# A two-layer trunk on one core: the norm's column sums behind the fourth product, half of the operand sums made as x tiles come, turns of h apart from their use, slots oldest first

## The chip, the core and the metric

The kernel runs on one core of a Trainium2 chip. A core has five engines that follow programs of their own and meet at semaphores: TensorE (PE; its weight loads are listed as PEld), VectorE (DVE), ScalarE (ACT), GpSimd (POOL) and SyncE (SP), which here issues nearly all transfers. PE writes into eight banks of PSUM, each 128 partitions by 512 fp32. The metric is the device time of one execution in microseconds (us), lower is better.

## The reference

The input x is 512 positions by 1024 channels, fp32. Two layers follow each other, and a norm ends the program:

```
for layer in range(2):
    h = rmsnorm(x, norm_mix_g[layer])
    x = x + (rglru_mixer(h) if layer == 0 else stick_breaking(h))      # both end with @ w_out
    h = rmsnorm(x, norm_ffn_g[layer])
    x = x + (silu(h @ w_gate) * (h @ w_up)) @ w_down                   # d_ff = 2816
return rmsnorm(x, final_g)
rmsnorm(x, g) = x * rsqrt(mean(x*x, channels) + 1e-6) * g
```

The mixer of layer 0 is a gated linear recurrence with a short convolution; that of layer 1 is attention with 16 heads in blocks of 128 queries.

## The kernel before

**Layout.** x lies transposed in SBUF as eight tiles x_1 to x_8 of 128 channels by 512 positions. Each large matmul in fp32 accuracy is made of three: the high part of one operand (rounded, `wh`, `oh`, `hh`, `uh`) by the high part of the other, high by low and low by high (the low parts `wl`, `ol`, `hl`, `ul` are what the rounding left). Weights come in chunks of 128x1024 from HBM by SP; ACT casts a chunk to its high part (L233), DVE or POOL subtracts to get the low part (L234). Three pairs of buffers and a fourth for every fourth chunk hold them.

**FFN.** `ffn` (L590) works on units of 512 columns of gate and up, u = 0 to 5, the last with 256. A unit is computed by a scheme of seven products in place of eight (in the order 1, 5, 6, 3, 7, 2, 4), each of two chunks and 24 matmuls. The products need sums and differences: of the weights (`source`, L76, made by DVE from the pieces `raw` and `b`, results `tt` or `b` itself), and of the quarters of x (`ffn_in`, L328). For m < 4, `ffn_in` makes one operand tile, for m >= 4 it scales x_(m-3) and x_(m+1) on ACT (L344, L345), makes four sums of 256 columns on DVE (L346, L331), and three high and low parts (L353, L331). `ffn_in` runs for each x tile as the mixer's out product delivers it: PE fills a bank, DVE adds it to x (L585 in layer 0, L970 in layer 1), then the operands are made. `norm_sq` (L371) squares the tile on ACT and adds it to `acc`, on POOL, the last one on DVE. `norm_rs1` sums acc's columns with four small matmuls (L389) and makes the factor rsT, which is needed only where product 2 is scaled (L690).

**h.** A unit's result h lies in the tiles u2 and b5 (L691, L697). In the next unit, `turn` transposes it: for two f tiles, eight transposes into banks 6 and 7 (L627), a copy to hh on ACT (L630), hl on DVE (L631). Then four `down_pair`s (L647) of 24 matmuls (L640 to L642) each use all four hh and hl, go to the banks 6 and 7, and DVE adds these to two x tiles (L645). In unit u the order is: product 1, turn(0,1), product 5, turn(2,3), pair 0, product 6, pair 1, product 3, pair 2, product 7, pair 3, products 2 and 4. In the last unit pairs 2 and 3 are replaced by work behind the units: two down chunks into four banks, turn(0,1) of the last h, then two short chunks that finish the x tiles.

**What sets the order.** PE's order in `ffn` is as written. The orders of DVE, ACT and POOL in `ffn` and in RG-LRU come from a scheduler, so that a change of PE's text moves rows on other engines; attention is written out by hand. Two scratch lists, `free` and `free2`, hand out slots of 128x512 (`new`, `rel`): the main list is served first, in order of release. The table in `plan` sets the order in which SP loads the chunks and the splitting follows. `finish` (L400) ends the program in two halves of the positions: last x add, square, column sums (L411), factor, output.

Of the kernel before, what the change touches and what calls it, by code (L numbers as in the profile page):

```python
# [97 lines left out]
class Kern:  # L98
    def __init__(self, ctx, tc, a, out):
# [6 lines left out]
        self.free = deque(range(NS1))  # L106
        self.free2 = deque()
        self.keep2 = 0
# [15 lines left out]
    @contextmanager  # L124
    def stage(self, name):
        with self.tc.tile_pool(name=name, bufs=1) as self.ar2:
            self.free2 = deque(range(NS1, NS1 + NS2))
            yield
            assert len(self.free2) == NS2
            self.free2 = deque()  # L130

    def new(self, name, dt=F32, second=False, shape=None):
        if second and self.free2:
            i = self.free2.popleft()
        elif self.free or len(self.free2) <= self.keep2:
            i = self.free.popleft()
        else:
            i = self.free2.popleft()
        self.tn += 1
        ar = self.ar if i < NS1 else self.ar2  # L140
        t = ar.tile(shape or [P, S], dt, tag=f"s{i}", bufs=1, name=f"{name}_{self.tn}")
        self.slot[id(t)] = (i, t)
        return t

    def rel(self, *ts_):
        for t in ts_:
            i = self.slot.pop(id(t))[0]
            (self.free if i < NS1 else self.free2).append(i)
# [5 lines left out]
    def plan(self):  # L154
# [173 lines left out]
    def ffn_in(self, m, g):  # L328
# [3 lines left out]
        if m == 0:  # L332
            self.ops = [None] * 4
        if m < 4:
            t = self.new("a11", F32R)
            nc.scalar.activation(t[:, lo], self.x[m][:, lo], AF.Copy, scale=self.col(g, m))
            nc.vector.scalar_tensor_tensor(t[:, hi], self.x[m][:, lo], self.col(g, m), t[:, lo].bitcast(F32),
                                           ALU.mult, ALU.subtract)
            self.ops[m] = {1: (t[:, lo], t[:, hi])}
            self.held.append(t)  # L340
        else:
            k = m - 4
            ua, ub, w1, w2 = (self.tmp() for _ in range(4))
            nc.scalar.activation(ub, self.x[m], AF.Copy, scale=self.col(g, m))  # L344
            nc.scalar.activation(ua, self.x[k], AF.Copy, scale=self.col(g, k))  # L345
            nc.vector.tensor_tensor(w1[:, lo], ua[:, hi], ub[:, hi], ALU.add)  # L346
# [3 lines left out]
            for src, q0, q1 in ((w1, 5, 6), (w2, 7, 3), (ub, 2, 4)):  # L350
                h, l = self.new("oh", F32R), self.new("ol", F32R)
                self.held += [h, l]
                nc.scalar.copy(h, src)  # L353
                sub(l, src, h.bitcast(F32))
                self.ops[k][q0] = (h[:, lo], l[:, lo])
                self.ops[k][q1] = (h[:, hi], l[:, hi])
        self.norm_sq(m)
# [74 lines left out]
    def rglru(self):  # L432
        nc, tc = self.nc, self.tc
        with ExitStack() as cx:
# [146 lines left out]
            ys = list(zip(ah, al))  # L581
            for m in range(KT):
# [7 lines left out]
    def ffn(self, l, gnext):  # L590
        nc, tc = self.nc, self.tc
        mm = nc.tensor.matmul
        with tc.tile_pool(name=f"ffn{l}", bufs=1) as self.fp, tc.manual_schedule(engines={mybir.EngineType.PE}):
# [30 lines left out]
            def turn(fs, banks):  # L624
                for f, b in zip(fs, banks):
                    for t in range(NT):
                        nc.tensor.transpose(b[:, ts(t)], (u2 + b5)[t][:, ts(f)], self.ident)  # L627
                    h, lw = (self.fp.tile([P, S], F32R, tag=f"{n}{f}", bufs=1, name=f"{n}{f}_{self.used}")
                             for n in ("hh", "hl"))
                    nc.scalar.copy(h, b)  # L630
                    nc.vector.tensor_tensor(lw, b, h.bitcast(F32), ALU.subtract)  # L631
                    hh[f] = (h, lw)
# [20 lines left out]
            for u in range(NU + 1):  # L653
                un = self.unit_of()
                w = un.w
                A, B, D = (ab[(u + i) % 3] for i in range(3))
# [18 lines left out]
                if 0 < u < NU:  # L675
                    down_pair(1)
# [3 lines left out]
                if u > 0:  # L680
                    down_pair(2 if u < NU else 1)
# [3 lines left out]
                if 0 < u < NU:  # L685
                    down_pair(3)
# [7 lines left out]
                for j in range(2):  # L694
# [3 lines left out]
                                                   ALU.mult, ALU.mult)  # L698
            self.rel(*self.held)
            self.held = []  # L700
            open_ = {4: tb[0], 5: tb[1], 6: B[0], 7: B[1]}
            w = self.chunk()
            for i in range(2):
                down(w, i, 4, open_[4 + i], last=False)
            save = hh[:]
            split7 = gnext is None
            w = self.chunk()
            hs = (slice(0, HS), slice(HS, S))
            p7 = (B[1], D[0])
            if split7:  # L710
                down(w, 0, 4, open_[6], last=False)
                for p, cs in zip(p7, hs):
                    down(w, 1, 4, p, last=False, cs=cs)
            else:
                for i in range(2):
                    down(w, i, 4, open_[6 + i], last=False)
            turn((0, 1), (A[0], A[1]))
            if gnext is None:
                with tc.issue_after(self.last.ins):
                    nc.scalar.activation(self.st[:, 0:1], self.ones[:, 0:1], AF.Sqrt)  # L720
            fin = [D[1], A[0], A[1], D[1]] if split7 else [D[0], D[1], A[0], A[1]]
            for e in range(2):
                w = self.chunk()
                for i in range(4):
                    m = 4 * e + i
                    if m == KT - 1 and split7:
                        for j in range(2):
                            down(w, i, 2, p7[j], first=False, cs=hs[j])
                            self.bi = 4 + 2 * j
# [5 lines left out]
                    self.norm_in(m, gnext)  # L735
# [374 lines left out]
```

## Time and profile before

| | us |
|---|---|
| median of 3 runs (lowest, highest) | 1240.68 (1239.98, 1242.27) |
| the profiled execution | 1241.45 |
| its span | 1239.7 |
| PE busy, share of the span | 1149.1, 93% |
| DVE busy | 878.8, 71% |
| ACT busy | 640.5, 52% |
| POOL busy | 349.4, 28% |
| one middle unit of the FFN (307 to 371 us): PE busy of 64 us | 62.48 |

The mean granted clock of PE is 0.969 of full speed. The span by stage: RG-LRU up to about 165 us, FFN of layer 0 up to 530, attention up to 850, FFN of layer 1 up to 1218, final norm to the end. In the time line, a row gives start, length, engine, line, operation, output<-inputs, shapes, and in brackets how long the engine stood before it and what ended that. Lengths of neighbouring rows overlap a little, since an engine starts an instruction before the one ahead has retired.

### The profile page before, as it was taken

What the parts mean: (1) busy time and instruction counts of PE and PEld (TensorE: products, weight loads), DVE (VectorE), ACT (ScalarE), POOL (GpSimd) and SP (SyncE); (2) the same over time, 40 slices, a digit from 0 to 9 for tenths busy, and PEclk for the clock granted to TensorE, in tenths of its full rate; (3) what the DMA queues carried; (4) which work ended last, traced back from release to release, by engine and by line L of the source; (5) the groups of instructions that cost most, each with busy time, mean ns of one, the idle gap of its engine ahead of it and who ended that gap; (6) DMA issues with size and microseconds to landing.
All of it is one profiled execution on the core that took longest, in us unless ns stands there. A gap on an engine that the chain in (4) does not pass through costs nothing. (4 is left out here: it accounts for less than half of the span.)

```text
span 1239.7 us, 14201 instructions
## 1 busy us (share of the span) xinstructions
PE 1149.1 (93%) x5363; PEld 946.8 (76%) x5363; DVE 878.8 (71%) x1105; ACT 640.5 (52%) x919; POOL 349.4 (28%) x218
## 2 busy tenths in 40 slices
PE   9999959999999999999989888797999999999995
PEld 6877848787878788888767677675878787878884
DVE  7878696756575756454899999969675757575744
ACT  6697464535353534344677777646353535353432
POOL 2541410111111111351466566621011111111134
PEclk9999989999999999999999999898999999999997
DMA  7223333232324131322111100023324241422101
GB/s 239 85 84 94 109 105 104 83 120 71 134 68 136 68 102 51 103 85 69 51 37 50 34 35 35 34 87 118 102 72 132 68 136 68 137 68 102 51 17 68
DMA packets 30740, 105.83 MB, mean 85 GB/s; under 512 B 3536, under 2 KB 4560, under 8 KB 30672
## 3 DMA queue, kind: packets, MB, share of 16 engines
q1 hardware_dynamic: 30384, 104.40, 25.2%
q8 instruction: 42, 0.69, 0.2%
q10 hardware_dynamic: 288, 0.52, 0.1%
q14 instruction: 26, 0.21, 0.1%
HBM read 102.81 MB, written 2.10 MB: 85 GB/s over the span
## 5 line engine op out<-in xcount | busy, mean ns | idle before, releaser
L234 POOL TENSOR_TENSOR wl<-raw,wh 128x1024 fp32r<-128x1024 f32 (+1 forms) x74 | 180.8, 2443 | 694.6 <-ACT wh L233 692.3
L233 ACT CAST wh<-raw 128x1024 fp32r<-128x1024 f32 (+1 forms) x154 | 156.0, 1017 | 198.6 <-PE bank L622 93.8
L620 PE MATMUL bank<-wh,oh 128*128 128x512 f32 (+1 forms) x576 | 217.0, 377 | 0.0
L621 PE MATMUL bank<-wl,oh 128*128 128x512 f32 (+1 forms) x576 | 215.7, 375 | 0.0
L622 PE MATMUL bank<-wh,ol 128*128 128x512 f32 (+1 forms) x576 | 215.6, 374 | 0.0
L640 PE MATMUL bank<-hh,wh 128*128 128x512 f32 (+1 forms) x358 | 139.9, 391 | 15.6 <-DVE hl L631 15.1
L645 DVE TENSOR_TENSOR x<-x,bank 128x512 f32<-128x512 f32 x87 | 59.7, 686 | 114.5 <-PE bank L642 113.4
L641 PE MATMUL bank<-hl,wh 128*128 128x512 f32 (+1 forms) x358 | 138.6, 387 | 0.4 <-DVE hl L631 0.4
L642 PE MATMUL bank<-hh,wl 128*128 128x512 f32 (+1 forms) x358 | 138.4, 387 | 0.0
L234 DVE TENSOR_TENSOR wl<-raw,wh 128x1024 fp32r<-128x1024 f32 (+1 forms) x80 | 102.1, 1280 | 45.3 <-ACT wh L233 45.2
L622 PEld LDWEIGHTS bank<-wh,ol 128*128 128x128 f32 x576 | 109.6, 190 | 19.3
L620 PEld LDWEIGHTS bank<-wh,oh 128*128 128x128 f32 x576 | 109.8, 191 | 18.8
L621 PEld LDWEIGHTS bank<-wl,oh 128*128 128x128 f32 x576 | 109.7, 190 | 19.0
L233 ACT CAST wh<-tt 128x1024 fp32r<-128x1024 f32 x66 | 69.5, 1053 | 93.2 <-PE bank L622 46.0
L233 ACT CAST wh<-b 128x1024 fp32r<-128x1024 f32 x44 | 46.4, 1053 | 127.6 <-PE bank L622 44.8
L267 PE MATMUL bank<-uh,wh 128*128 128x512 f32 x256 | 104.6, 409 | 6.8 <-DVE t L814 4.3
L268 PE MATMUL bank<-ul,wh 128*128 128x512 f32 x256 | 101.6, 397 | 0.3 <-DVE ul L323 0.3
L269 PE MATMUL bank<-uh,wl 128*128 128x512 f32 x256 | 101.3, 396 | 0.0
L234 DVE TENSOR_TENSOR wl<-tt,wh 128x1024 fp32r<-128x1024 f32 x66 | 80.9, 1225 | 22.0 <-ACT wh L233 21.7
L640 PEld LDWEIGHTS bank<-hh,wh 128*128 128x128 f32 x358 | 67.5, 189 | 31.5 <-DVE hl L631 17.5
L234 DVE TENSOR_TENSOR wl<-b,wh 128x1024 fp32r<-128x1024 f32 x44 | 53.9, 1224 | 41.8 <-ACT wh L233 41.2
L641 PEld LDWEIGHTS bank<-hl,wh 128*128 128x128 f32 x358 | 67.5, 189 | 14.3 <-DVE hl L631 1.1
(205 smaller groups left out, 2328.4 us busy)
## 6 DMA issues: line engine op xcount, KB each, us to landing
raw<-w_gu SPq DMA_DIRECT2D x44, 512.0 KB, 3.5
b<-w_gu SPq DMA_DIRECT2D x44, 512.0 KB, 3.5
raw<-w_dn SPq DMA_DIRECT2D x44, 512.0 KB, 3.5
raw<-w_qk SPq DMA_DIRECT2D x16, 512.0 KB, 3.4
raw<-w_in SPq DMA_DIRECT2D x14, 512.0 KB, 3.9
raw<-w_ao SPq DMA_DIRECT2D x8, 512.0 KB, 3.9
raw<-w_v SPq DMA_DIRECT2D x8, 512.0 KB, 3.5
raw<-w_bo SPq DMA_DIRECT2D x8, 512.0 KB, 3.5
```

The costliest lines, as they stand in the source:

```text
L233: self.nc.scalar.copy(wh[:, c], raw[:, c])
L234: self.wl_engine(i).tensor_tensor(wl[:, c], raw[:, c], wh[:, c].bitcast(F32), ALU.subtract)
L267: mm(out, lhsT=wh, rhs=xh, start=first, stop=False)
L268: mm(out, lhsT=wh, rhs=xl, start=False, stop=False)
L269: mm(out, lhsT=wl, rhs=xh, start=False, stop=last)
L620: mm(out[j][:, :w], lhsT=oh[:, ts(j)], rhs=wh[:, ws], start=st, stop=False, skip_group_check=True)
L621: mm(out[j][:, :w], lhsT=oh[:, ts(j)], rhs=wl[:, ws], start=False, stop=False, skip_group_check=True)
L622: mm(out[j][:, :w], lhsT=ol[:, ts(j)], rhs=wh[:, ws], start=False, stop=en, skip_group_check=True)
L640: mm(out, lhsT=w[0][:, ws], rhs=h[:, cs], start=st, stop=False, skip_group_check=True)
L641: mm(out, lhsT=w[0][:, ws], rhs=lw[:, cs], start=False, stop=False, skip_group_check=True)
L642: mm(out, lhsT=w[1][:, ws], rhs=h[:, cs], start=False, stop=en, skip_group_check=True)
L645: nc.vector.tensor_tensor(self.x[m], self.x[m], bank, ALU.add)
```

## The change

1. `norm_rs1` of unit 0 stands behind product 3, the fourth, and no longer behind product 1.
2. `ffn_in` makes half of the operand sums of product 7 for m < 4, and from m = 4 on three 256-wide sums and one half-wide low part. It scales the older x tile first, and takes its tiles from the main list. All additions to acc go to POOL, in the last norm to DVE.
3. From unit 2 on, turn(0,1) stands ahead of product 1 and turn(2,3) behind it; pair 3 goes behind product 4, ahead of that turn. Pairs 1 and 2 go behind products 3 and 7. Unit 1 keeps its turns. The last turn(0,1) goes between the two down chunks, into tiles of its own. The table of chunks follows.
4. Out tiles of attention use bank m for tile m, and the three pairs of banks of the products are shifted by one pair in layer 1.
5. Slots carry the time of their release; of the two lists the one with the older slot is served.

```diff
-    def new(self, name, dt=F32, second=False, shape=None):
-        if second and self.free2:
-            i = self.free2.popleft()
-        elif self.free or len(self.free2) <= self.keep2:
-            i = self.free.popleft()
+    def new(self, name, dt=F32, second=False, shape=None, first=False):
+        two = not first and len(self.free2) > (0 if second else self.keep2)
+        if two and (second or not self.free or self.free2[0][0] < self.free[0][0]):
+            i = self.free2.popleft()[1]
         else:
-            i = self.free2.popleft()
+            i = self.free.popleft()[1]
...
-                    order = (0, 1, d[0], 2, d[1], 3, d[2], 4, d[3], 5, 6)
+                    order = (0, 1, d[0], 2, 3, d[1], 4, d[2], 5, 6, d[3])
...
+        def split(dst, src):
+            h, l = dst
+            nc.scalar.copy(h, src)
+            sub(l, src, h.bitcast(F32))
+
         if m < 4:
-            t = self.new("a11", F32R)
-            nc.scalar.activation(t[:, lo], self.x[m][:, lo], AF.Copy, scale=self.col(g, m))
-            nc.vector.scalar_tensor_tensor(t[:, hi], self.x[m][:, lo], self.col(g, m), t[:, lo].bitcast(F32),
-                                           ALU.mult, ALU.subtract)
-            self.ops[m] = {1: (t[:, lo], t[:, hi])}
...
+            ua, w2 = self.tmp(), self.tmp()
+            t, t3 = self.new("a11", F32R, first=True), self.new("s3", F32R, first=True)
+            nc.scalar.activation(ua, self.x[m], AF.Copy, scale=self.col(g, m))
+            sub(w2[:, lo], ua[:, lo], ua[:, hi])
+            self.ops[m] = {1: (t[:, lo], t[:, hi]), 7: (t3[:, lo], t3[:, hi])}
+            split(self.ops[m][1], ua[:, lo])
+            split(self.ops[m][7], w2[:, lo])
         else:
...
+            nc.scalar.activation(ua, self.x[k], AF.Copy, scale=self.col(g, k))
             nc.scalar.activation(ub, self.x[m], AF.Copy, scale=self.col(g, m))
-            nc.scalar.activation(ua, self.x[k], AF.Copy, scale=self.col(g, k))
             nc.vector.tensor_tensor(w1[:, lo], ua[:, hi], ub[:, hi], ALU.add)
             sub(w1[:, hi], w1[:, lo], ua[:, lo])
-            sub(w2[:, lo], ua[:, lo], ua[:, hi])
...
+            split((h1, l1), w1)
             sub(w2[:, hi], ub[:, lo], w1[:, hi])
...
+            split(self.ops[k][3], w2[:, hi])
+            split((h2, l2), ub)
-        self.norm_sq(m)
+        self.norm_sq(m, nc.gpsimd)
...
+            self.bi = 0
             for m in range(KT):
...
-                A, B, D = (ab[(u + i) % 3] for i in range(3))
+                A, B, D = (ab[(u + i + l) % 3] for i in range(3))
+                if u > 1:
+                    turn((0, 1), tb)
                 product(1, un, A, 0)
...
-                if u == 0:
-                    self.bi = 6
-                    self.norm_rs1(False)
-                else:
-                    turn((0, 1), tb)
+                if u > 0:
+                    turn((0, 1) if u == 1 else (2, 3), tb)
                 product(5, un, B, 0)
-                if u > 0:
+                if u == 1:
                     turn((2, 3), tb)
...
-                if 0 < u < NU:
-                    down_pair(1)
                 product(3, un, B, 0, False)
...
                 if u > 0:
-                    down_pair(2 if u < NU else 1)
+                    down_pair(1)
+                if u == 0:
+                    self.bi = 6
+                    self.norm_rs1(False)
                 product(7, un, A, 0, False)
...
                 if 0 < u < NU:
-                    down_pair(3)
+                    down_pair(2)
                 product(2, un, D, 0)
...
+                if 0 < u < NU:
+                    down_pair(3)
...
             for i in range(2):
                 down(w, i, 4, open_[4 + i], last=False)
-            save = hh[:]
...
+            nh = [(self.new("h4", F32R), self.new("l4", F32R)) for _ in range(2)]
+            turn((0, 1), (A[0], A[1]), nh)
             w = self.chunk()
...
-                    self.norm_in(m, gnext)
+                    if split7:
+                        self.norm_sq(m, nc.vector)
+                    else:
+                        self.norm_in(m, gnext)
```

Three places of DVE's order show what the scheduler makes of it. The first is behind the last x add of layer 0's mixer, where the last operands and the first weights of product 5 are made (t, ol, ow: sums and low parts of the operands; tt: weight sum; wl: its low part). Before:

```order
L331 TENSOR_TENSOR t_1438<-t_1435 128x256
L331 TENSOR_TENSOR t_1437<-t_1437,t_1435 128x256
L331 TENSOR_TENSOR ol_1454<-t_1436,oh_1453 128x512
L76 TENSOR_TENSOR tt_1485<-b_178_1473,raw_1244 128x1024
L331 TENSOR_TENSOR t_1438<-t_1436,t_1437 128x256
L76 TENSOR_TENSOR tt_1503<-b_179_1475,raw_1300 128x1024
L234 TENSOR_TENSOR wl_1488<-tt_1485,wh_1487 128x1024
L331 TENSOR_TENSOR ol_1446<-t_1437,oh_1445 128x512
```

Now:

```order
L332 TENSOR_TENSOR ow_1468<-t_1458,ow_1467 128x512
L332 TENSOR_TENSOR t_1460<-t_1458,t_1459 128x256
L332 TENSOR_TENSOR ow_1466<-t_1459,ow_1465 128x512
L76 TENSOR_TENSOR tt_1505<-b_186_1493,raw_1272 128x1024
L332 TENSOR_TENSOR ow_1469<-t_1460,ow_1469 128x256
L76 TENSOR_TENSOR tt_1523<-b_187_1495,raw_1326 128x1024
L235 TENSOR_TENSOR wl_1508<-tt_1505,wh_1507 128x1024
```

Two 512-wide low parts stand ahead of the first weight sum, where there was one, and none is left behind wl.

The second is the start of unit 3 of layer 0: the last h tile (b), the last two x adds, the first turn's hl. Before:

```order
L697 SCALAR_TENSOR_TENSOR b_1471<-b_1471,rsT,t_2629 128x512
L76 TENSOR_TENSOR tt_2635<-b_223_2573,tt_2635 128x1024
L234 TENSOR_TENSOR wl_2656<-tt_2653,wh_2655 128x1024
L697 SCALAR_TENSOR_TENSOR b_1472<-b_1472,rsT,t_2632 128x512
L76 TENSOR_TENSOR tt_2653<-b_224_2597,tt_2653 128x1024
L234 TENSOR_TENSOR wl_2709<-tt_2635,wh_2708 128x1024
L631 TENSOR_TENSOR hl_80_2678<-bank_76,hh_80_2677 128x512
L631 TENSOR_TENSOR hl_80_2686<-bank_77,hh_80_2685 128x512
```

Now:

```order
L706 SCALAR_TENSOR_TENSOR b_1491<-b_1491,rsT,t_2617 128x512
L235 TENSOR_TENSOR wl_2672<-tt_2669,wh_2671 128x1024
L706 SCALAR_TENSOR_TENSOR b_1492<-b_1492,rsT,t_2620 128x512
L654 TENSOR_TENSOR x_7_84<-x_7_84,bank_76 128x512
L76 TENSOR_TENSOR tt_2669<-b_231_2585,tt_2669 128x1024
L654 TENSOR_TENSOR x_8_85<-x_8_85,bank_77 128x512
L235 TENSOR_TENSOR wl_2690<-tt_2687,wh_2689 128x1024
L639 TENSOR_TENSOR hl_78_2658<-bank_76,hh_78_2657 128x512
L639 TENSOR_TENSOR hl_78_2666<-bank_77,hh_78_2665 128x512
```

The two x adds of pair 3 have come between b and hl, with a weight sum between them.

The third is unit 1, whose turns keep their place. Before:

```order
L631 TENSOR_TENSOR hl_44_1822<-bank_77,hh_44_1821 128x512
L76 TENSOR_TENSOR tt_1771<-raw_1931,tt_1771 128x1024
L234 TENSOR_TENSOR wl_1880<-tt_1789,wh_1879 128x1024
L631 TENSOR_TENSOR hl_46_1865<-bank_76,hh_46_1864 128x512
L631 TENSOR_TENSOR hl_46_1873<-bank_77,hh_46_1872 128x512
```

Now:

```order
L639 TENSOR_TENSOR hl_44_1842<-bank_77,hh_44_1841 128x512
L76 TENSOR_TENSOR tt_1789<-raw_1933,tt_1789 128x1024
L235 TENSOR_TENSOR wl_1898<-tt_1807,wh_1897 128x1024
L76 TENSOR_TENSOR tt_1807<-raw_1951,tt_1807 128x1024
L235 TENSOR_TENSOR wl_1930<-b_199_1729,wh_1929 128x1024
L639 TENSOR_TENSOR hl_46_1883<-bank_76,hh_46_1882 128x512
L639 TENSOR_TENSOR hl_46_1891<-bank_77,hh_46_1890 128x512
```

One weight sum and one low part more stand ahead of the second turn's hl.

More of the change, by code (lines that the diff above doesn't have):

```diff
@@ L105, in __init__ @@
         self.ar = mk("ar", 1)
-        self.free = deque(range(NS1))
+        self.free = deque((0, i) for i in range(NS1))
         self.free2 = deque()
+        self.clock = 0
         self.keep2 = 0
@@ L126, in stage @@
         with self.tc.tile_pool(name=name, bufs=1) as self.ar2:
-            self.free2 = deque(range(NS1, NS1 + NS2))
+            self.free2 = deque((0, i) for i in range(NS1, NS1 + NS2))
             yield
@@ L704, in ffn @@
                 down(w, i, 4, open_[4 + i], last=False)
-            save = hh[:]
-            split7 = gnext is None
+            nh = [(self.new("h4", F32R), self.new("l4", F32R)) for _ in range(2)]
+            turn((0, 1), (A[0], A[1]), nh)
             w = self.chunk()
[L708 to L721, printed above, removed]
+            down(w, 0, 4, open_[6], last=False)
+            for p, cs in zip(p7, hs) if split7 else ((open_[7], slice(0, S)),):
+                down(w, 1, 4, p, last=False, cs=cs)
+            hh[:2] = nh
+            fin = [D[1], A[0], A[1], D[1] if split7 else D[0]]
             for e in range(2):
```

35 lines of the change are left out of this document (21 added, 14 removed).

## The prediction

> **What bounds the kernel now.** I read the page first: one engine is busy nearly all the time.
>
> ```profile
> span 1239.7 us, 14201 instructions
> PE 1149.1 (93%) x5363; PEld 946.8 (76%) x5363; DVE 878.8 (71%) x1105; ACT 640.5 (52%) x919; POOL 349.4 (28%) x218
> ```
>
> TensorE (PE) bounds the kernel. The change keeps the number of its matmuls, so only what PE loses between them can be won: idle time, and time at half its clock. The view of waits says who ends the idle time (total, times, longest, in us); the window below it is attention.
>
> ```profile
> PE bank L389 <- DVE acc L371: 17.9, 2, 13.2
> PE bank L640 <- DVE hl L631: 15.1, 10, 1.5
> PE bank L627 <- DVE b L697: 4.9, 4, 1.6
> PE bank L620 <- DVE x L970: 4.3, 1, 4.3
> ...
> 530.00:795.00 265.00, 238.88 (x1163) 193.06 (x1161) 226.28 (x316) 181.17 (x304) 144.52 (x104) 0.96 0.15 50
> ```
>
> The first row is the norm's column sums, twice; the second and third are the turns of h, spread over five units of two layers; the fourth is the first product of layer 1. Together they are 42 of the 90.6 us (1239.7 less 1149.1) that PE is not busy. Another 26 (265 less 238.88) lie in attention, where the written order is untouched. Last I read the time lines of PE and DVE around each wait. Behind product 1 of layer 0 (start, length; in brackets the idle time before and what ended it):
>
> ```profile
> 165.31 0.39 PE L620 MATMUL bank<-wh,a 128*128 128x512 f32 x1
> 170.52 0.39 PE L622 MATMUL bank<-wh,a 128*128 128x512 f32 x1
> 184.06 1.86 PE L389 MATMUL bank<-ones,acc 128*128 128x1 f32 x8 [13.15 <-DVE acc L371]
> 185.79 0.77 PE L620 MATMUL bank<-wh,oh 128*128 128x512 f32 x1
> 193.76 0.39 PE L620 MATMUL bank<-wh,oh 128*128 128x512 f32 x1
> ...
> 163.48 0.68 DVE L585 TENSOR_TENSOR x<-x,bank 128x512 f32<-128x512 f32 x1
> 167.25 1.52 DVE L331 TENSOR_TENSOR t<-t,t 128x256 f32<-128x256 f32 x1
> 170.07 0.68 DVE L585 TENSOR_TENSOR x<-x,bank 128x512 f32<-128x512 f32 x1
> 172.22 0.43 DVE L346 TENSOR_TENSOR t<-t,t 128x256 f32<-128x256 f32 x1 [1.47 <-ACT t L345]
> 173.83 1.22 DVE L76 TENSOR_TENSOR tt<-b,raw 128x1024 f32<-128x1024 f32 x1
> 176.44 1.22 DVE L234 TENSOR_TENSOR wl<-tt,wh 128x1024 fp32r<-128x1024 f32 x1
> 182.18 1.22 DVE L234 TENSOR_TENSOR wl<-tt,wh 128x1024 fp32r<-128x1024 f32 x1
> 183.31 0.69 DVE L371 TENSOR_TENSOR acc<-acc,t 128x512 f32<-128x512 f32 x1
> ```
>
> PE stands from 170.9 to 184.06 until DVE's last addition to acc, which sits behind a queue of weight sums. But the first weights of product 5 are complete only at 176.44+1.22 = 177.7: a wait of 6.8 us hides behind the norm's. And the whole queue is late: PE had finished out tile 7 by 165.31, yet its x add began at 170.07.
>
> **The two starts of the FFN.** Four parts of the change meet here. (1) The column sums go behind the fourth product, three products of 24 matmuls later. A product takes 5.45 us (24 steps from 165.31 to 170.75), so some 16 us pass in which acc gets done. The sums' own time stays. The eight rows took 1.73 (184.06 to 185.79) at half clock, at full clock they cannot take less than half of it, 0.87: I take 1.1. (2) For m >= 4, DVE makes three 256-wide sums where it made four, and a low part of 256 columns where it was 512. In its place ACT and DVE do more, smaller operations for m < 4, earlier, while out tiles still come. A 256-wide DVE operation is 0.43 by the 172.22 row, a 512-wide one 0.69: one sum and a quarter of a microsecond less, 0.6 to 0.7 per tile. DVE's last tiles come 6.6 us apart (163.48 to 170.07) against 5.45 for an out tile on PE, which is where the lateness is made. A sum may also escape POOL: the one at 167.25 took 1.52 beside a POOL addition to acc. Over the four tiles I take 3 us, between 1.8 and 4.7, the whole lateness. (3) The last addition to acc goes from DVE to POOL, off the queue that makes weights. (4) In DVE's new order, shown above, one more low part (0.69) stands ahead of the first weight sum; against that ACT scales the older x tile before the last one has come, half of the 1.47 in which DVE waited for ACT's two scalings. This cancels.
>
> The chain, then: x add at about 167; first weight sum 3.8 us later as before (170.07 to 173.83), at 170.9; its low part starts 2.6 us after it (173.83 to 176.44, with ACT's cast between) and takes 1.2: done at 174.7. If POOL's addition meets the weight sum, add 1.1 (1.52 less 0.42). The Trainium skill, "SBUF — State Buffer", section "Who interferes with whom", speaks against moving the addition: a VectorE instruction with two SBUF inputs and a GpSimd instruction that reads SBUF lock each other out for a whole instruction. By that rule the start is 175.8; the 1.52 row agrees with it.
>
> Product 5 starts near 174.7 then, not at 185.79, with a gap of about 4 us left (170.9 to 174.7). Product 6 needs five more weight operations and its own low part on DVE, six steps of 1.13 (182.18 to 183.31), 6.9 us with their signals: it starts at 181.6, where it began at 193.76. That late start also carries the half clock (the third number from the end is the granted clock):
>
> ```profile
> 185.00:194.00 9.00, 9.00 (x31) 7.34 (x31) 6.33 (x11) 1.90 (x3) 0.00 (x0) 0.67 0.00 0
> ```
>
> 0.67 over 9 us is 5.9 us at half clock, 3 us lost. The gap of 4 may cost as much again, or nothing. So 12.2, less 1.1 for the sums, less 1 for the clock: **10 us**, bounds 7 (POOL's 1.1 and the clock's 3) and 11. The Trainium skill, "TensorE: Matmul & The Clock Gate", Part 1, says that one idle window of about 3.4 us throttles for at least a window: an estimate by it is 1.7 us lost and not 1. The trace agrees so far that the clock fell behind the gap of 13.
>
> Layer 1 has the same queue and one wait more: product 1 itself stood for the x add of out tile 7, which used its bank.
>
> ```profile
> 853.33 0.68 DVE L970 TENSOR_TENSOR x<-x,bank 128x512 f32<-128x512 f32 x1
> 854.16 0.77 PE L620 MATMUL bank<-wh,a 128*128 128x512 f32 x1 [4.31 <-DVE x L970]
> 859.70 1.22 DVE L234 TENSOR_TENSOR wl<-tt,wh 128x1024 fp32r<-128x1024 f32 x1
> 867.33 1.86 PE L389 MATMUL bank<-ones,acc 128*128 128x1 f32 x8 [4.74 <-DVE acc L371]
> 876.76 0.39 PE L620 MATMUL bank<-wh,oh 128*128 128x512 f32 x1
> ```
>
> The banks are shifted, so product 1 follows at 849.85 (854.16 less 4.31) and ends at 855.3. The x add can be at 850.9, not before 849.9; the chain of 7.6 us (853.33 to 860.92) gives product 5 at 858.5 and, 6.9 later, product 6 at 865.4, against 876.76. 11.4 less 1.1, less 1.5 for the clock: **8.8 us**, bounds 6 and 10.5.
>
> **The turns.** At a middle unit the transposes and the first use of hl lie so:
>
> ```profile
> 288.96 0.76 DVE L697 SCALAR_TENSOR_TENSOR b<-b,rsT,t 128x512 f32<-128x512 f32 x1
> 291.65 0.38 PE L627 MATMUL bank<-ident,u 128*128 128x128 f32 x2
> 291.87 0.38 PE L627 MATMUL bank<-ident,b 128*128 128x128 f32 x2
> 299.79 1.29 DVE L631 TENSOR_TENSOR hl<-bank,hh 128x512 fp32r<-128x512 f32 x2 [0.86 <-ACT hh L630]
> 300.54 0.50 PE L640 MATMUL bank<-hh,wh 128*128 128x512 f32 x1 [1.52 <-DVE hl L631]
> ```
>
> From unit 2 on, a whole product stands between the second turn and the down pair that uses it, so the 1.52 goes. The first turn stands ahead of product 1, right behind the moved last down pair, and its transposes into bank 7 wait for the x add that empties that bank: 0.69 and about 0.1 for the signals behind the last matmul, less four transposes into bank 6 at 0.11. That is 0.4; I take 0.5. L76 stands between the two x adds on DVE, in the 2.7 us that half a pair takes on PE, so it should be over. The b rows are ready: product 1's 24 steps before the transposes began at 291.65 - 5.45 = 286.2, b was ready at 289.7, and the down pair now fills 5.45. So 1.0 for units 2 to 4 in two layers: 6.1. Unit 5 has two waits today, and the last turn one:
>
> ```profile
> 480.75 0.33 PE L627 MATMUL bank<-ident,b 128*128 128x128 f32 x1 [0.89 <-DVE b L697]
> 486.74 0.50 PE L640 MATMUL bank<-hh,wh 128*128 128x512 f32 x1 [1.47 <-DVE hl L631]
> 524.35 0.50 PE L640 MATMUL bank<-hh,wh 128*128 128x512 f32 x1 [0.24 <-ACT hh L630]
> ```
>
> Unit 5's 2.36 becomes 0.5, 1.86 twice: 3.7. The last turn goes between two down chunks and saves 0.24 twice: 0.5. Unit 1 keeps its place, but not its queue:
>
> ```profile
> 234.79 1.04 ACT L233 CAST wh<-raw 128x1024 fp32r<-128x1024 f32 x1 [1.71 <-PE bank L622]
> 236.35 1.29 DVE L631 TENSOR_TENSOR hl<-bank,hh 128x512 fp32r<-128x512 f32 x2 [2.02 <-ACT hh L630]
> ```
>
> The low part of that cast was POOL's, since it was a down chunk; in the new chunk order a gate-up piece stands here, DVE makes its low part, and ahead of hl: 235.83 to 237.0. Hl starts 0.7 later, a loss of 1.4 in two layers. The turns in sum: 6.1 + 3.7 + 0.5 - 1.4 = **8.9 us**, bounds 0 (the new wait as long as the old ones) and 11.
>
> **The rest.** At the end the additions to acc go from POOL to DVE; in RG-LRU, DVE does a gt row ahead of its scans for which PE stood 2.18:
>
> ```profile
> 1212.80 8.11 POOL L371 TENSOR_TENSOR acc<-acc,t 128x512 f32<-128x512 f32 x6
> 1218.71 0.63 ACT L369 ACTIVATE t<-x 128x512 f32<-128x512 f32 x1 [0.73 <-DVE x L645]
> 1220.96 0.27 PE L411 MATMUL bank<-ones,acc 128*128 128x1 f32 x1 [2.36 <-POOL acc L371]
> 110.71 0.47 PE L267 MATMUL bank<-uh,wh 128*128 128x512 f32 x1 [2.18 <-DVE gt L566]
> ```
>
> POOL's six take 1.35 each, one behind the other. The last square ends at 1219.34, and a DVE addition takes 0.69: 1220.1 in place of 1220.96, **0.85** saved, bounds 0 and 1. Of the 2.18, the low part of the weights behind the scans keeps some: **0.7**, bounds 0 and 1.5. The slots (which freed buffer a new tile takes): no row charges a wait of PE to a slot, 0, bounds -1 and 2.
>
> Sum: 10 + 8.8 + 8.9 + 0.85 + 0.7 = 29.25. The profiled execution took 1241.45 (its span and 1.75 around it); that leaves 1212.2. The median of the runs is 0.77 lower than that execution, so **1211 us**.
>
> **The rivals.** *The weights take the norm's place.* If DVE's queue does not come forward, product 5 waits until 177.7 and 860.9, as the low parts do today, and the clock falls: then 5.5 and 6 us and not 18.8, and 1211 + 7 = 1218. For it: DVE is the queue that all of this passes through. Against: less work stands in it. *The turns' wait only moves.* If DVE is in a 1.2 us weight sum when bank 7 must be emptied, the new gap is about 1.7 and the turns give nothing: 1220. *Slots make it slower.* Attention has 16 heads and DVE is busy 226 of its 265 us; if the oldest slot is one that a late reader still holds, every head pays. It decides from 30 us, 1.9 per head; at 2.2 (35 us) the time is 1246. Against: the longest freed slot is the likeliest to be done with. *The change doesn't do it:* PE still waits for acc behind the fourth product, and 18.8 us stay: 1230. acc would have to come 9 us later than 184, which no row suggests.
>
> **Chances.** Forecast, 1206 to 1217: 0.62; weights 0.17; turns 0.13; the norm still waiting 0.03; slots 0.05. The range 1203 to 1224 takes in the first two rivals and a better start (the lateness gone whole, 2 us in attention). A measurement here tells 0.2%, 2.5 us, from no change: faster 0.94, same 0.02, slower 0.04.
>
> **What would show it.** Right: no wait ahead of the column sums, a gap of about 4 us ahead of product 5, waits for hl at unit 1 alone, and 0.5 us for an x add inside the first turns. Wrong: a gap of 7 us ahead of product 5 or a new one ahead of product 6; over 1 us inside the first turns; more idle time of PE in attention.

## The result and the profile after

The changed kernel takes 1212.8 us (median of 4 runs, 1211.94 to 1213.82) against 1241.38 for the kernel before on the same chip: a ratio of 0.9771, 95% interval 0.9754 to 0.9788. The forecast was 1211, range 1203 to 1224. One of the executions below, the profiled one of the kernel with the old operand sums, was disturbed (2278.81 us), so that kernel's time is the median of its other three and no trace of it is read. The page and those waits of PE after the change that bear on the FFN and the end (total, times, longest, in us; rows of attention and of RG-LRU between them are left out; lines have moved: L635 is the transposes, L649 the first down matmul, L628 the products, L396 the column sums of the FFN's norm, L418 those of the final norm):

```profile
span 1211.5 us, 14202 instructions
PE 1143.9 (94%) x5363; PEld 940.4 (78%) x5363; DVE 887.8 (73%) x1117; ACT 648.6 (54%) x935; POOL 342.0 (28%) x214
...
PE bank L628 <- ACT wh L234: 6.1, 2, 3.3
...
PE bank L649 <- DVE hl L639: 4.3, 2, 2.2
...
PE bank L635 <- DVE b L706: 3.1, 2, 1.6
...
PE bank L635 <- DVE x L654: 2.7, 8, 0.3
...
PE bank L629 <- DVE wl L235: 1.9, 2, 1.0
...
PE bank L418 <- DVE acc L378: 1.6, 1, 1.6
```

The 17.9 us for acc ahead of the FFN's column sums are gone, and so is the 4.3 us for the x add in layer 1. In their place stands a wait for the first weights of product 5 (wh, then wl), 8 us in the two layers. The 15.1 us for hl have become 4.3, at unit 1 alone, and eight waits of 0.34 for an x add have come inside the first turns. The time lines of PE, DVE and POOL at the start of layer 0's FFN:

```profile
175.44 0.68 PE L628 MATMUL bank<-wh,ow 128*128 128x512 f32 x1 [2.87 <-ACT wh L234]
176.97 0.80 PE L629 MATMUL bank<-wl,ow 128*128 128x512 f32 x1 [0.85 <-DVE wl L235]
184.87 0.39 PE L628 MATMUL bank<-wh,ow 128*128 128x512 f32 x1
195.76 0.95 PE L396 MATMUL bank<-ones,acc 128*128 128x1 f32 x8
...
168.19 0.68 DVE L593 TENSOR_TENSOR x<-x,bank 128x512 f32<-128x512 f32 x1
172.01 2.30 DVE L76 TENSOR_TENSOR tt<-b,raw 128x1024 f32<-128x1024 f32 x1
175.70 1.21 DVE L235 TENSOR_TENSOR wl<-tt,wh 128x1024 fp32r<-128x1024 f32 x1
...
171.88 1.34 POOL L378 TENSOR_TENSOR acc<-acc,t 128x512 f32<-128x512 f32 x1 [2.39 <-ACT t L376]
```

Product 5 starts at 175.44 and product 6 (the third PE row) at 184.87. The first weight sum (L76) takes 2.30 us, where one without company takes 1.22: it starts while POOL's addition to acc runs (171.88 to 173.22) and ends 1.09 behind it. Behind the gap PE ran product 5 mostly at half clock (granted clock 0.76 over 170 to 184, 6.7 us at half), so that it came to product 6 only at 184.87, although the first low part for it was complete at 183.72 (182.51 and 1.21).

The wait for b at unit 1, which the change leaves as it was, looks like a meeting of the same two engines. The rows of the second b and of POOL's low part of a down chunk:

```profile
217.57 2.88 DVE L706 SCALAR_TENSOR_TENSOR b<-b,rsT,t 128x512 f32<-128x512 f32 x1
217.12 2.79 POOL L235 TENSOR_TENSOR wl<-raw,wh 128x1024 fp32r<-128x1024 f32 x1 [43.89 <-ACT wh L234]
```

The first b takes 0.75. In the kernel before it was the same: 2.87 beside 2.78 on POOL.

Cut at landmarks of PE, the two executions compare so (us; the row of unit 1 runs to the point where only its own work is done):

| stage | before | after | saved | foretold |
|---|---|---|---|---|
| start to product 1 of layer 0 | 165.31 | 166.97 | -1.7 | 0.7 |
| product 1 to the first turn, layer 0 | 61.10 | 51.49 | 9.6 | 10 |
| unit 1, layer 0 | 59.79 | 62.04 | -2.25 | -0.7 |
| units 2 to 5 and the last turn, layer 0 | 249.8 | 242.85 | 7.0 | 5.15 |
| attention to the end of its out product | 313.8 | 311.9 | 2.0 | 0 |
| from there to the first turn, layer 1 | 59.6 | 52.0 | 7.6 | 8.8 |
| unit 1, layer 1 | 59.79 | 62.07 | -2.3 | -0.7 |
| units 2 to 5 and the last turn, layer 1 | 249.4 | 242.4 | 7.0 | 5.15 |
| the end | 21.1 | 19.9 | 1.2 | 0.85 |

### The profile page after: what moved, and what is told of

It reads as the page before. It is cut to its first block, busy times and chain, and to the rows that moved or that the text cites. A ratio compares the mean times of both kernels' runs of the same rounds, so it can differ in the third digit from the quotient of the medians.

```text
span 1211.5 us, 14202 instructions
## 1 busy us (share of the span) xinstructions
PE 1143.9 (94%) x5363; PEld 940.4 (78%) x5363; DVE 887.8 (73%) x1117; ACT 648.6 (54%) x935; POOL 342.0 (28%) x214
## 4 chain that ended last, share of the span: by engine, by line
PE 62%; DVE 22%; issue 4%; ACT 4%; POOL 0%; DVEq 0%; ACTq 0%; POOLq 0%
PE bank L629 10%; PE bank L630 10%; PE bank L628 10%; PE bank L649 7%; PE bank L651 7%; PE bank L650 7%; DVE wl L235 4%; PE bank L268 3%; PE bank L269 3%; PE bank L270 3%; DVE sph L887 3%; DVE t L886 2%; DVE r L893 1%; PE bank L635 1%; ACT wh L234 1%
## 5 line engine op out<-in xcount | busy, mean ns | idle before, releaser
L628 PE MATMUL bank<-wh,ow 128*128 128x512 f32 (+1 forms) x480 | 181.5, 378 | 6.1 <-ACT wh L234 6.1
L629 PE MATMUL bank<-wl,ow 128*128 128x512 f32 (+1 forms) x480 | 180.8, 377 | 1.9 <-DVE wl L235 1.9
L630 PE MATMUL bank<-wh,ow 128*128 128x512 f32 (+1 forms) x480 | 180.4, 376 | 0.0
L235 DVE TENSOR_TENSOR wl<-raw,wh 128x1024 fp32r<-128x1024 f32 (+1 forms) x80 | 105.2, 1317 | 43.7 <-ACT wh L234 43.5
L649 PE MATMUL bank<-hh,wh 128*128 128x512 f32 (+1 forms) x324 | 126.9, 392 | 4.3 <-DVE hl L639 4.3
L650 PE MATMUL bank<-hl,wh 128*128 128x512 f32 (+1 forms) x324 | 126.6, 391 | 0.0
L651 PE MATMUL bank<-hh,wl 128*128 128x512 f32 (+1 forms) x324 | 126.5, 391 | 0.0
L628 PEld LDWEIGHTS bank<-wh,ow 128*128 128x128 f32 x480 | 91.7, 191 | 22.9 <-ACT wh L234 7.0
L629 PEld LDWEIGHTS bank<-wl,ow 128*128 128x128 f32 x480 | 91.8, 191 | 18.5 <-DVE wl L235 2.7
L630 PEld LDWEIGHTS bank<-wh,ow 128*128 128x128 f32 x480 | 91.8, 191 | 16.0
L888 POOL TENSOR_TENSOR spl<-t,sph 128x512 fp32r<-128x512 f32 (+1 forms) x48 | 59.0, 1234 | 58.3 <-DVE sph L887 46.1
L649 PEld LDWEIGHTS bank<-hh,wh 128*128 128x128 f32 x324 | 61.6, 190 | 17.2 <-DVE hl L639 4.8
```

The costliest lines, as they stand in the source:

```text
L235: self.wl_engine(i).tensor_tensor(wl[:, c], raw[:, c], wh[:, c].bitcast(F32), ALU.subtract)
L628: mm(out[j][:, :w], lhsT=oh[:, ts(j)], rhs=wh[:, ws], start=st, stop=False, skip_group_check=True)
L629: mm(out[j][:, :w], lhsT=oh[:, ts(j)], rhs=wl[:, ws], start=False, stop=False, skip_group_check=True)
L630: mm(out[j][:, :w], lhsT=ol[:, ts(j)], rhs=wh[:, ws], start=False, stop=en, skip_group_check=True)
L649: mm(out, lhsT=w[0][:, ws], rhs=h[:, cs], start=st, stop=False, skip_group_check=True)
L650: mm(out, lhsT=w[0][:, ws], rhs=lw[:, cs], start=False, stop=False, skip_group_check=True)
```

## The experiments

My theory of the result: the FFN's two starts (17 us) are bound by DVE's weight queue, the column sums only sat on top of it; the turns give 14 us less the 4.5 that unit 1 loses. The rival for the starts: it was the place of the column sums in PE's order. All kernels were timed against the kernel before on their chip (1241.7 to 1242.3 us).

**The column sums put back.** In the changed kernel `norm_rs1` returns behind product 1:

```diff
                 if u > 0:
                     turn((0, 1) if u == 1 else (2, 3), tb)
+                else:
+                    self.bi = 6
+                    self.norm_rs1(False)
...
-                if u == 0:
-                    self.bi = 6
-                    self.norm_rs1(False)
                 product(7, un, A, 0, False)
```

> The changed kernel (1212.8 us) with the norm's column sums put back behind product 1; POOL still makes the last addition to acc. Theory 'weights': in the changed kernel acc is complete at 173.2 us, and product 5 starts at 175.44 because its first weights are not ready, so the sums fit into that gap: 1212 to 1216 us, and the gap ahead of product 5 stays 3 to 5 us. Rival 'place': the place of the column sums was the wait; then PE stands 8 us or more in each layer again, 1228 us or more.

Measured: 1211.94 us, ratio 0.9761 (0.9745 to 0.9777). The first part of the change can be undone for nothing. The time line of PE in that kernel:

```profile
173.44 1.05 PE L396 MATMUL bank<-ones,acc 128*128 128x1 f32 x8 [0.68 <-POOL acc L378]
175.60 0.49 PE L628 MATMUL bank<-wh,ow 128*128 128x512 f32 x1 [1.11 <-ACT wh L234]
177.13 0.80 PE L629 MATMUL bank<-wl,ow 128*128 128x512 f32 x1 [1.03 <-DVE wl L235]
```

The sums fit into the gap in which PE waits for weights. They still wait 0.68 for acc, and it costs nothing: product 5 starts at 175.60.

**The last addition put back too.** Beside the edit above, DVE adds the last square again:

```diff
-        self.norm_sq(m, nc.gpsimd)
+        self.norm_sq(m)
```

> As before it, and the last addition to acc goes to DVE again, so both are undone. The scheduler puts that addition right behind the first low part of product 5. Theory 'weights': acc at about 177.6, column sums then, product 5 near 179: 3 to 5 us lost per layer, 1219 to 1223 us. Rival 'place': 13 us of standing as before the change, 1231 us or more.

Measured: 1213.16 us, 0.9772 (0.9757 to 0.9787). Both theories were too dear. The scheduler now puts the addition right behind the first low part and no longer behind six more rows, so PE's wait for acc is 3.9 us and not 13. With both parts of the norm undone the kernel is as fast as with both: these two edits together earn nothing. Which of them helps and which harms, the next run tells.

**The last addition alone.** The same two lines as the only edit: column sums behind product 3, addition on DVE.

> The changed kernel with only the last addition to acc back on DVE, the column sums behind product 3. In the changed kernel the first weight sum took 2.30 us in place of 1.22, beside POOL's addition. Theory 'lock': without POOL's addition it takes 1.22, product 5 starts 1.1 us earlier and product 6 about 0.4 earlier (DVE has 0.6 more to do): 1211 to 1213 us. Rival 'queue': the added 0.69 on DVE's queue costs as much per layer and more: 1214 us or more.

Measured: 1206.77 us, 0.9731 (0.9708 to 0.9754), faster than the changed kernel by 6 us. In DVE's time line of this kernel the weight sum has its own length, and the addition follows the low part:

```profile
171.11 1.22 DVE L76 TENSOR_TENSOR tt<-b,raw 128x1024 f32<-128x1024 f32 x1
173.72 1.22 DVE L235 TENSOR_TENSOR wl<-tt,wh 128x1024 fp32r<-128x1024 f32 x1
174.85 0.68 DVE L378 TENSOR_TENSOR acc<-acc,t 128x512 f32<-128x512 f32 x1
...
173.46 0.49 PE L628 MATMUL bank<-wh,ow 128*128 128x512 f32 x1 [1.77 <-ACT wh L234]
```

The gap of PE falls from 2.87 to 1.77, by the 1.1 that the weight sum is shorter. Product 6 gains another 0.9: it starts 8.5 us behind product 5 here and 9.4 in the changed kernel (175.44 to 184.87). That goes with the clock: behind the shorter gap PE was at half clock for 3.4 us (0.83 over 172 to 182), in the changed kernel for 6.7. The stage from product 1 to the first turn falls from 51.5 to 49.45 in layer 0 and from 52.0 to 49.7 in layer 1, 4.3 of the 7.0 us between the two profiled executions (1213.29 and 1206.26); 1.6 more are half clock at unit 1 of layer 1, which this execution did not have. The meeting of POOL and DVE was foreseen, its price set too low. The four kernels together show that the two edits for the norm depend on each other (medians, us):

| | last addition on DVE | on POOL |
|---|---|---|
| column sums behind product 1 | 1213.16 | 1211.94 |
| column sums behind product 3 | 1206.77 | 1212.8 |

Moving the sums earns 6.4 us with the addition on DVE and nothing with it on POOL. Moving the addition to POOL costs 6 us with the sums behind product 3, and about nothing with them behind product 1.

**The old operand sums.** The changed kernel with the old `ffn_in` (tiles from the main list, additions to acc on POOL as in the change):

```diff
-            nc.vector.tensor_tensor(w1[:, lo], ua[:, hi], ub[:, hi], ALU.add)
...
+            sub(w2[:, lo], ua[:, lo], ua[:, hi])
             sub(w2[:, hi], ub[:, lo], w1[:, hi])
+            for src, q0, q1 in ((w1, 5, 6), (w2, 7, 3), (ub, 2, 4)):
```

> The changed kernel (1212.8 us) with the old operand sums, column sums behind product 3, last addition on POOL. Theory 'two cures for one wait': the sums' place holds most of the gain without the new operands, x adds come some 3 us later and product 6 1 to 2 us later per layer: 1214 to 1218 us. Rival 'the operands carry the gain': 8 us per layer are lost, 1226 us or more.

Measured: 1215.73 us, 0.9791 (0.9775 to 0.9807). The operands alone are worth 3 us here, far from the 17 of the starts. So neither part, taken away alone, costs much. That is what two cures of one wait would look like; the proof is to give each alone to the kernel before.

**Each cure alone.** First the kernel before with nothing but the column sums moved behind product 3:

```diff
-                if u == 0:
-                    self.bi = 6
-                    self.norm_rs1(False)
-                else:
+                if u > 0:
                     turn((0, 1), tb)
...
+                if u == 0:
+                    self.bi = 6
+                    self.norm_rs1(False)
                 product(7, un, A, 0, False)
```

> The kernel before (1241.4 us) with one part of the change alone: the column sums behind product 3; DVE still makes the last addition to acc, the operands are the old ones. Theory 'two cures for one wait': the sums' move alone lets product 5 start when its first weights are ready, near 177 us in place of 185.8, product 6 near 184 in place of 193.8; 8 us per layer, 1225 us, between 1222 and 1229. Rival 'the move is worth nothing' (its undoing cost the changed kernel nothing): 1239 to 1242 us.

Measured: 1226.5 us, 0.9879 (0.9864 to 0.9894). Then the kernel before with nothing but the new operand sums (the new `ffn_in` word for word, with its tiles from the main list, but with `self.norm_sq(m)` at its end):

> The kernel before with the other part alone: the new operand sums of ffn_in; the column sums behind product 1, the last addition on DVE. The scheduler now puts that addition right behind the first low part of product 5 and not behind seven more operations. Theory 'two cures for one wait': the wait of 13 us falls to about 4 as in the changed kernel with both norm parts undone, 9.5 us in layer 0 and 7 in layer 1: 1225 us, between 1222 and 1228. Rival 'operands save only their own DVE time', 3 us per layer: 1235 us.

Measured: 1222.57 us, 0.9839 (0.9816 to 0.9862). Alone they save 15.8 and 19.7 us; together they cannot save 35, because the wait is there once. In the two starts of the FFN (the second and the sixth row of the table) the move of the sums alone saves 8.1 and 9.1 us, the operands alone 9.7 and 9.9, the whole change 9.6 and 7.6, and the change with the last addition on DVE 11.6 and 9.9. PE's time line says what is left in each, first with the column sums moved alone, then with the new operands alone:

```profile
177.90 0.80 PE L620 MATMUL bank<-wh,oh 128*128 128x512 f32 x1 [5.27 <-ACT wh L233]
```

```profile
176.35 1.86 PE L397 MATMUL bank<-ones,acc 128*128 128x1 f32 x8 [3.90 <-DVE acc L379]
```

The move of the sums uncovers the weights (5.27, the wait that I had read as hidden behind the norm's). The new operands bring the queue forward and, through the scheduler, the addition to acc with it: 3.90 in place of 13.15. That the addition moved ahead of six DVE rows was in the order of the instructions, and I had not asked which edit had moved it.

**The banks of layer 1.** The changed kernel without the shift:

```diff
-                A, B, D = (ab[(u + i + l) % 3] for i in range(3))
+                A, B, D = (ab[(u + i) % 3] for i in range(3))
```

> The changed kernel without the shift of the banks in layer 1, so that product 1 there waits for the x add of out tile 7 again (some 2.2 us). Theory 'weights': product 5 waits 3 us for its weights behind product 1 anyway, so the wait only moves: 1212 to 1214 us. Rival: the wait and its half clock add 2 to 4 us: 1215 to 1217 us.

Measured: 1211.31 us, 0.9754 (0.9738 to 0.977). Product 1 waits again, and product 5 hardly does:

```profile
835.93 0.77 PE L628 MATMUL bank<-wh,a 128*128 128x512 f32 x1 [2.26 <-DVE x L983]
843.36 0.50 PE L628 MATMUL bank<-wh,ow 128*128 128x512 f32 x1 [0.26 <-ACT wh L234]
```

The weights' due time decides, and the shift earns nothing.

**The turns.** The changed kernel with the units' old order, and the old order of chunks; the last turn stays new:

```diff
-                    order = (0, 1, d[0], 2, 3, d[1], 4, d[2], 5, 6, d[3])
+                    order = (0, 1, d[0], 2, d[1], 3, d[2], 4, d[3], 5, 6)
...
-                if u > 1:
-                    turn((0, 1), tb)
```

> The changed kernel with the turns, down pairs and the chunk order inside the units as before the change; the last turn keeps its new place. In units 2 to 5 this gives back 1.22 us three times and about 2.5 us in unit 5 per layer; at unit 1 it wins back 2.25 us per layer that the changed chunk order lost. Theory 'turns as costed': 1212.8 + 12.4 - 4.5 = 1220.7, between 1219 and 1223 us. Rival 'turns give little': 1214 to 1216 us.

Measured: 1220.77 us, 0.9835 (0.982 to 0.9849), where 1220.7 was expected. The turns are the part that is worth what they were said to be: 8 us net.

**Unit 1.** The low part that stands ahead of hl goes to POOL, one chunk per layer:

```diff
+            if isinstance(e, Piece) and e.unit.u == 1 and e.q == 3 and e.c == 0:
+                return self.nc.gpsimd
```

> The changed kernel (1212.8 us) with the low part of one chunk per layer (product 3's first in unit 1, the one that stands ahead of the second turn's hl) made by POOL and not by DVE. Theory 'queue': the wait ahead of unit 1's first down pair falls from 2.17 to 1.52 us, and the half clock behind it stays away: 0.65 to 2.2 us per layer, 1208.5 to 1211.5 us. Rival 'chance': the 2.17 is not from that low part; 1212 to 1213.5 us.

Measured: 1208.73 us, 0.9736 (0.972 to 0.9751). Unit 1 takes 59.8 us again in both layers, as before the change. First the rows of the changed kernel, with the window behind the wait (third number from the end: the granted clock), then the same of this one:

```profile
227.93 1.22 DVE L235 TENSOR_TENSOR wl<-b,wh 128x1024 fp32r<-128x1024 f32 x1 [0.28 <-ACT wh L234]
229.08 1.28 DVE L639 TENSOR_TENSOR hl<-bank,hh 128x512 fp32r<-128x512 f32 x2
229.81 0.50 PE L649 MATMUL bank<-hh,wh 128*128 128x512 f32 x1 [2.17 <-DVE hl L639]
228.00:238.00 10.00, 8.19 (x29) 6.61 (x30) 3.73 (x5) 2.85 (x5) 0.00 (x0) 0.83 0.16 52
```

```profile
227.80 1.29 DVE L642 TENSOR_TENSOR hl<-bank,hh 128x512 fp32r<-128x512 f32 x2 [0.76 <-ACT hh L641]
228.55 0.50 PE L652 MATMUL bank<-hh,wh 128*128 128x512 f32 x1 [1.52 <-DVE hl L642]
227.00:237.00 10.00, 8.48 (x38) 7.00 (x38) 3.93 (x6) 3.29 (x6) 2.38 (x1) 1.00 0.17 54
```

One low part of 1.2 us makes the wait 0.65 longer, as foretold, and this longer wait was followed by half clock (0.83 over 10 us is 3.4 us at half, 1.7 lost); 1.52 was not.

**Unit 1 with cover.** Its first down pair goes behind product 6, the chunk with it:

```diff
+                if u == 1:
+                    order = (0, 1, 2, d[0], 3, d[1], 4, d[2], 5, 6, d[3])
...
-                if u > 0:
+                if u > 1:
                     down_pair(0)
...
+                if u == 1:
+                    down_pair(0)
                 product(3, un, B, 0, False)
```

> The changed kernel with unit 1's first down pair behind product 6 and not behind product 5, its chunk moved with it. Theory 'cover': a product now stands between the second turn and the use of hl, as in the other units, so the wait of 2.17 us and the half clock behind it (0.8 us on average) go in both layers: 1207 us, between 1205 and 1209. Rival 'next wait': product 6 itself or the pair waits for weights that the moved chunk has pushed back: 1211 us or more.

Measured: 1209.98 us, 0.9739 (0.9724 to 0.9754), a smaller gain than expected. The wait for hl is gone, but the new chunk order has put two low parts between the two b rows, where the change has none, and the first turn waits longer for b:

```profile
216.96 2.35 DVE L237 TENSOR_TENSOR wl<-tt,wh 128x1024 fp32r<-128x1024 f32 x2
219.23 0.74 DVE L710 SCALAR_TENSOR_TENSOR b<-b,rsT,t 128x512 f32<-128x512 f32 x1
...
220.03 0.33 PE L637 MATMUL bank<-ident,b 128*128 128x128 f32 x1 [2.60 <-DVE b L710]
```

2.60 in place of 1.55, although b itself now takes 0.74 and no longer 2.88 (POOL's low part has moved away). In layer 0 half clock followed (0.83 over 219 to 229), in layer 1 it did not (1.00 over 886 to 896). The rival had it right that the moved chunk pushes something back, but named another place.

**Both together.** The addition on DVE (`self.norm_sq(m)`) and the edit just shown:

> The changed kernel with the last addition to acc on DVE (alone: 1206.8 us) and unit 1's first down pair behind product 6. The two lie at different places, so both gains should stand: 1201 us, between 1199 and 1204. If it is above 1206, they share a cause.

Measured: 1205.17 us, 0.9702 (0.9688 to 0.9716), the fastest kernel of this study, 7.6 us below the change. It is 4.2 above the 1201 expected; 3 of these are what unit 1 had already failed to give by itself (1209.98 for 1207). With the gains of the two alone, 6.0 and 2.8, the sum would be 1204.0. Behind the waits for b half clock followed in both layers here (0.83 over 217 to 227 and over 882 to 892). The addition on DVE with the POOL low part of unit 1 was not tried.

**The slots.** The changed kernel with the lists as before:

```diff
-        if two and (second or not self.free or self.free2[0][0] < self.free[0][0]):
-            i = self.free2.popleft()[1]
+        if second and self.free2:
+            i = self.free2.popleft()
+        elif self.free or len(self.free2) <= self.keep2:
```

> The changed kernel with slots as before: the main list first, in its own order. The rows of DVE in RG-LRU then stand as before the change. Theory 'slots moved both': RG-LRU wins back the 1.1 us it lost (new gap of 1.12 at 125.4 us, less what the gt row saves) and attention loses the 2.1 us it won: 1213 to 1215 us. Rival 'attention won from the banks or from chance': 1211 to 1212 us.

Measured: 1211.85 us, 0.976 (0.9744 to 0.9775), where the rival had it. RG-LRU did not get its microseconds back: DVE's order there is the old one again, PE waits 2.18 for gt as before the change, and yet product 1 starts at 166.89. The window from 104 to 118 us shows why, the kernel before first, then this one:

```profile
104.00:118.00 14.00, 11.82 (x52) 9.47 (x52) 14.00 (x19) 9.87 (x15) 0.58 (x1) 1.00 0.23 76
```

```profile
104.00:118.00 14.00, 11.82 (x45) 9.28 (x44) 14.00 (x19) 8.24 (x13) 0.00 (x0) 0.88 0.25 76
```

The same wait, once at full clock behind it and once not: 0.88 over 14 us is 3.4 us at half clock, 1.7 us. So the old order reaches product 1 at 165.31 without such a piece and at 166.89 with one. The change reaches it at 166.97 without one (its clock is 1.00 from 5 to 166 us): it is slower there than the old order at its best, and no better than the old order with the piece. The medians, 1211.85 and 1212.8, don't tell the two orders apart. In attention the kernel with the old slots takes 313.55, close to the old 313.8, while the change takes 311.9. But the kernel with the column sums put back has the change's attention and takes 313.35. So the 2 us are not the slots' either, as far as these runs can tell; what they come from stays open.

## Why the prediction was right, point by point

**The size and the sign** held: 1211 foretold, 1212.8 measured. That the sum came so close is in part luck: in the table, five stages saved 7.2 us less than foretold and four saved 6.1 us more. The signs named ahead were all there: no wait ahead of the column sums, gaps of 3.7 and 4.3 us ahead of product 5 (about 4 foretold), waits for hl at unit 1 alone, 0.34 for an x add inside the first turns.

**The starts of the FFN** (10 and 8.8 foretold, 9.6 and 7.6 measured). The chain was right: the weights of product 5 take the place of the norm as the wait, they were to be complete 7.6 us behind the last x add, and were (168.19 to 176.91 is 8.7, with POOL's 1.1 that had been put in the bounds). What failed is the share of the four parts. Part (1), the column sums' move, was the first reason given; in the changed kernel it earns nothing, with the addition on DVE 6.4 us, alone on the old kernel 15.8. Part (2) was costed by its own DVE time, 0.6 us a tile; alone on the old kernel it does the whole, since with it the scheduler moves the addition to acc forward too. Part (3), the addition on POOL, was taken as a relief of DVE's queue; with the sums behind product 3 it costs 2 us per layer. The bank shift of layer 1, whose wait of 4.3 was counted as won, earns nothing: product 5 cannot start before its weights, at 843.91 with the shift and at 843.36 without it.

The Trainium skill's rule ("SBUF — State Buffer", "Who interferes with whom"), that a VectorE instruction with two SBUF inputs and a GpSimd instruction that reads SBUF lock each other out, agrees with the traces: 2.30 with the addition beside it, 1.22 without.

**The turns** (8.9 foretold, 9.5 measured: 7.0 less 2.25 in each layer). The step for units 2 to 4 was right; the new gap, 0.5 estimated, was 0.34, which gives 1.22 a unit and not 1.0. Unit 5 and the last turn gave 3.3 a layer, not 2.1. Unit 1's term was mis-sized: the 0.7 was right (0.65), the half clock behind it was missing, 1.6. That part is chance: the kernels with the old slots and with the old banks keep the wait of 2.17, and in layer 0 their clock stayed up behind it and unit 1 took 60.4 us, not 62.0.

**The rest.** The end gave 1.2 for 0.85. RG-LRU's 0.7 failed, and so did its lower bound of 0: the gt row no longer delays PE by 2.18, but a low part behind the scans does by 1.05 and another row (al) by 1.12, and the profiled execution reached product 1 1.7 later. Attention, put at nothing, came out 2.0 shorter; no run shows why.

**The rivals.** "The weights take the norm's place" came true as a wait and not as a price: DVE's queue did come forward. "The turns' wait only moves" is refuted by the eight waits of 0.34, "the norm still waiting" by the missing row. That slots slow the kernel by the 30 us and more that would have decided is refuted by the run without them (1211.85).

## What to carry to other kernels

Two edits that shorten the same wait don't add: 15.8 and 19.7 us alone, and 17 at that place for the whole change; taking one out of the finished kernel then shows little, so each must also be tried alone on the old one. When an edit on one engine lets a scheduler reorder another, look up which edit moved the row that PE waits for before giving each a share. An addition moved to an idle engine isn't free if it makes the busy one slower beside it (1.22 to 2.30 us here). It is worth looking for rows of the busy engine that take longer than their kind: the b row of 2.88 us at unit 1, on which PE waits 1.55 in both kernels, is still there, and no run tried to move POOL's low part away from it alone.

## What the runs showed of the hardware

The clock of PE falls in pieces of about 3.4 us also behind waits well shorter than that, and not each time: behind a wait of 2.18 us it stayed at 1.00 in one execution and went to 0.88 over the window of 14 us in another that waits for the same row; behind 2.17 us at unit 1 it fell in both layers of the change, and in layer 0 but not in layer 1 with the addition on DVE (0.83 over 225 to 235 us, 1.00 over 892 to 902). Behind the ten waits of 1.5 in the kernel before it did not fall (1.00 from 228 to 525 and from 915 to 1215 us). The Trainium skill, "TensorE: Matmul & The Clock Gate", Part 1, gives about one idle window of 3.4 us as what throttles, and says that the window runs freely; the second agrees with the chance seen here, the first is too long by these runs. So a wait of 2 us can cost 1.7 us more than its length, and stage times of single executions scatter by as much. It can be more: behind a wait of 1.85 in attention of the change, which ended at 604.03, the clock was 0.79 over 600 to 616 us, 6.7 us at half.
